# Attention by two key tiles, finer steps of maxima and recurrence, and TensorE's instructions chained in program order

## The chip, the cores and the metric

The kernel runs as one program on one core of a Trainium2 chip. The metric is the device time of one execution in microseconds. TensorE multiplies matrices, VectorE and ScalarE work on elements, GpSimd (POOL) helps with some, and SyncE's queue issues the DMA transfers. Products land in PSUM, where the kernel holds eight tiles of 128 x 512 float32, called banks here; everything else lives in SBUF.

## The reference, cut to what matters

The model has two layers over 256 context and 1024 latent tokens. In each layer three token mixers read the same projected input: a Fourier mix, grouped-query attention (8 query heads, 2 key heads, width 64), and a gated linear recurrence (4 heads, 64 x 64 state) run forward and backward. Their outputs are concatenated and go through one output projection and a SwiGLU FFN.

```python
def attend(q, k, v):
    s = jnp.einsum('bkgqd,bksd->bkgqs', q, k).astype(jnp.float32) * (HEAD_DIM ** -0.5)
    p = jax.nn.softmax(s, axis=-1).astype(v.dtype)
    return jnp.einsum('bkgqs,bksd->bkgqd', p, v)

    ...
    for l in range(DEPTH):
        ...
        fx = fourier_mix(col(ux, OFF_FOURIER, FOURIER_W), w_four[l])
        ax, ac = attention_group(ux, uc, base_c, q_norm[l], k_norm[l], tabs, ctx_out)
        rx, rc = hgrn_group(ux, uc, base_c, lb_all[:, l], hg_norm[l], ctx_out)
        x = x + g_a * (jnp.concatenate([fx, ax, rx], axis=-1) @ w_out[l])
```

Context tokens attend to context only, latent tokens to both; in the second layer the context has no output.

## The kernel before, in words

Tokens are cut into three chunks: chunk 0 is the context (256), chunks 1 and 2 are 512 latent tokens each. `mixers` first runs the projections of a layer and then the stretch that the change is about: attention, with the recurrence (`hgrn`) and the Fourier mix (`fourier`) interleaved.

Attention works in units: a unit is a pair of heads `j` and a chunk of queries. Layer 0 has 12 units (four of them context units with two key tiles), layer 1 has 8; a latent unit has ten key tiles of 128. For each key tile and each of the two heads `a`, two products make the scores (`sc`, L622 and L623, a float32 value split in two parts), ScalarE takes the exponential (`p`, L625), and one tile later the values are weighted (`pv`, L631). A float32 product appears as two instructions. The two heads of a weighting write the two halves of 64 partitions of one bank, so each uses 64 of TensorE's 128 columns. After every second tile four products with 32 columns each collect the sums (`sm`, L636). `unit_finish` divides by the sums.

The exponent needs the row maximum in advance. `unit_prepare` loads the queries of a unit two units ahead (`qf`, L567), converts them (four ScalarE instructions, L577 and L578), and for each block of 128 queries and each head multiplies with all keys in three pieces of 512, 512 and 256 columns (`mx`, L588) and reduces each piece on VectorE (`mp`, L589). The maxima are transposed (`mt`, L596) and brought into the operand `Q2` by a DMA (L603).

`hgrn` builds the recurrence by seven levels of doubling. A level multiplies small blocks (`lp`, 64 rows by 64 columns, L789), merges the result under a mask (VectorE, L796), and scales `W` and the keys (L813, L815) for the next level. Layer 0 has a second group of blocks for the context. Then states are summed (`kdt`, `kv`, `ST`) and read out (`ho`, L858 and L861, `oss`).

PSUM has four tags of two banks each: `mm`, `sc`, `mx`, `pv`. The finishing sum (L652) and `mt` share `mx` with the maxima.

The order of the work: each generator yields at the ends of its steps, and the loop in `mixers` interleaves them: for every key tile one step of the maxima of a later unit (three pieces) and 1.1 or 1.07 steps of `other`, the chain of two `hgrn` and one `fourier`. This gives each instruction a place in program order. A scheduler that works with modelled times then orders each engine's instructions: where the next one in program order is not ready by its model, it takes a later one that is. So TensorE's order in the trace is not program order: pieces of the recurrence and maxima stand between the parts of attention. At run time each engine works through its list in that fixed order.

Of the kernel before, what the change touches and what calls it, by code (L numbers as in the profile page):

```python
# [87 lines left out]
DELAY = 1  # L88
ORDER = (2, 3, 4, 6, 7, 0, 1, 5)
RATE = (1.1, 1.07)  # L90
# [4 lines left out]
PREPSTEPS = (5,)  # L95
# [5 lines left out]
class Kern:  # L101
    def __init__(self, ctx, tc, I, C, out):
# [9 lines left out]
        self.n = 0  # L112
# [14 lines left out]

    def mm3(self, out, terms, first=True, last=True):

        n = len(terms)  # L130
        for i, (lh, ll, rh, rl) in enumerate(terms):
            self.nc.tensor.matmul(out, lh, rh, start=(first and i == 0), stop=False)  # L132
            self.nc.tensor.matmul(out, lh, rl, start=False, stop=False)  # L133
            self.nc.tensor.matmul(out, ll, rh, start=False, stop=(last and i == n - 1))  # L134
# [11 lines left out]
    def consts(self):  # L146
# [9 lines left out]
        nc.tensor.transpose(ptr[:, 0:16], cv, self.c["ident"][0:16, 0:16])  # L156
# [15 lines left out]
    def vectors(self):  # L172
# [24 lines left out]
        nc.tensor.transpose(ptr[:, 0:P], rows, self.c["ident"])  # L197
# [33 lines left out]
    def ada_first(self, l, tags):  # L231
# [5 lines left out]
        for k in range(KD):  # L237
            if k == EARLYK:
                self.early_slabs(l)
            for q in range(4):  # L240
                t = next(tag)
                w = self.t2(f"wa{l}_{k}_{q}", tag=t, bufs={"wa": WAB, "pa": PAB, "acc": ACB}[t])
                nc.sync.dma_start(out=w, in_=self.I["w_ada"][l, k * P:(k + 1) * P, q * 512:(q + 1) * 512])
                nc.tensor.matmul(acc[32 * q:32 * q + 32], self.sc32[:, k, :], w, start=(k == 0), stop=(k == KD - 1))
# [3 lines left out]
    def ada_sums(self, l, blocks, tags):  # L248
# [19 lines left out]
        for group in groups:  # L268
# [16 lines left out]
            for r, acc in enumerate(accs):  # L285
                nc.tensor.matmul(ps[32 * r:32 * r + 32], self.c["ones"][:, 0:32], acc)
# [7 lines left out]
    def ada_columns(self, l, ps, group):  # L294
# [5 lines left out]
        for b in range(4):  # L300
            nc.tensor.transpose(pt[:, b * P:(b + 1) * P], rowsb[:, b * P:(b + 1) * P], self.c["ident"])
# [35 lines left out]
    def first_chunk(self, ci, vec):  # L337
# [20 lines left out]
        for t, xt in enumerate(xs):  # L358
# [9 lines left out]
            nc.tensor.matmul(R[:, t * P:(t + 1) * P], rb, self.c["ident"])  # L368
        for d in range(KD):
            pt = self.ps("mm", f"xtp{ci}_{d}")  # L370
            for t, xt in enumerate(xs):
                nc.tensor.transpose(pt[:, t * P:(t + 1) * P], xt[d // 4][:, d % 4 * P:d % 4 * P + P], self.c["ident"])
# [22 lines left out]
    def square_sum(self, acc, ci):  # L395
        n = CHUNKS[ci][1]
        ss = self.ps("pv", f"ss{ci}")
        self.nc.tensor.matmul(ss[:, :n], self.c["ones"], acc[:, :n])
# [62 lines left out]
    def qk_norm_rope(self, l, nm, ci, t0, n, acc, done):  # L461
# [7 lines left out]
        def rest():  # L469
            ss = self.ps("mx", "qss")  # L470
            nc.tensor.matmul(ss[:, :n], self.c["blkq"], sq[:, :n])
# [86 lines left out]
    def unit_prepare(self, l, i, j, ci, ops):  # L558
# [37 lines left out]
        nc.tensor.transpose(pt[:2 * nt, 0:P], m, self.c["ident"])  # L596
# [9 lines left out]
    def unit_attend(self, l, j, ci, Q1, Q2):  # L606
# [3 lines left out]
        g = j // 2  # L610
        n = CHUNKS[ci][1]
        nk = 2 if ci == 0 else 10
        pv = self.ps("pv", f"pv{j}_{ci}")
        sm = self.ps("pv", f"sm{j}_{ci}")
        ps = []
        for kt in range(nk + 1):
            if kt < nk:
                ks = slice(kt * P, (kt + 1) * P)
                p = []
                for a in range(2):  # L620
                    sc = self.ps("sc", "sc")
                    nc.tensor.matmul(sc[:, :n], self.K1[g][:, ks], Q1[a], start=True, stop=False)  # L622
                    nc.tensor.matmul(sc[:, :n], self.K2[g][0:66, ks], Q2[a][0:66], start=False, stop=True)  # L623
                    pf = self.t2(f"p{a}", tag="pa", bufs=PAB)[:, :n]
                    nc.scalar.activation(out=pf, in_=sc[:, :n], func=AF.Exp, scale=0.125)  # L625
                    p.append(pf)
                ps.append(p)
            if kt:
                i = kt - 1
                for a in range(2):  # L630
                    nc.tensor.matmul(pv[64 * a:64 * a + 64, :n], self.V[:, i, 64 * g:64 * g + 64], ps[i][a], start=(i == 0), stop=(i == nk - 1))  # L631
                if i % 2:
                    for a in range(2):
                        for o in range(2):
                            r = 64 * a + 32 * o
                            nc.tensor.matmul(sm[r:r + 32, :n], self.c["first"], ps[i - 1 + o][a], start=(i == 1), stop=(i == nk - 1), tile_position=(0, r))  # L636
            if kt == DELAY and self.pending:
                self.pending()
                self.pending = None
            yield  # L640
        if self.pending:
            self.pending()
        pvs, sms = [self.t2(nm, tag="acc", bufs=ACB)[:, :n] for nm in ("pvs", "sms")]
        nc.scalar.copy(out=pvs, in_=pv[:, :n])
        nc.scalar.copy(out=sms, in_=sm[:, :n])
        self.pending = lambda: self.unit_finish(j, ci, pvs, sms)

    def unit_finish(self, j, ci, pvs, sms):
# [3 lines left out]
        nc.tensor.matmul(sm[:, :n], self.c["blk"], sms)  # L652
# [56 lines left out]
    def hgrn(self, l, j):  # L709
# [10 lines left out]

        def load(src, name, a=0):
# [12 lines left out]
        for ci in cis:  # L734
# [3 lines left out]
            for dr in range(2):  # L738
                v.tensor_tensor(out=W[ci][:, 1 - dr], in0=f[dr][:, a:a + n], in1=q[:, a:a + n], op=ALU.mult)

# [4 lines left out]
        def pairs(group, product, put):  # L745

            lp = [self.ps("mm", "lp").rearrange("p (c t) -> p c t", t=64) for _ in range(2)]
            for x, (ci, c) in enumerate(group):
# [3 lines left out]
                if x == 3:  # L752
                    yield
# [3 lines left out]
            yield  # L757
# [536 lines left out]
```

## Time and profile before

| | us |
|---|---|
| median of 3 runs | 3320.73 (3320.39 to 3325.08) |
| the profiled execution | 3320.49, of which span 3318.6 |
| TensorE busy | 3238.2 (98%), 17370 products |
| VectorE busy | 1698.8 (51%) |
| ScalarE busy | 1116.6 (34%) |

Times of the trace are counted from the span's start. Busy time of TensorE is the union of its instructions; their ends are modelled and overlap the next instruction's start, so the cost of an instruction in a stream is the distance from its start to the next start. "Idle before" names the time an engine did nothing before an instruction and what ended it. The attention stretch of layer 0 lies from 350.5 to 779 us, that of layer 1 from 2094.8 to 2471.9 us.

### The profile page before, as it was taken

To read this page: it belongs to the slowest core of one execution; us is meant where nothing else is said; L and a number is where in the kernel's file an instruction comes from. 1 tells how busy PE (TensorE), PEld (TensorE's weight loads), DVE (VectorE), ACT (ScalarE), POOL (GpSimd) and SP (SyncE) were. 2 spreads that over 40 slices of the span, in tenths; PEclk is the share of its full clock that TensorE was granted. 3 is DMA by queue.
4 is the path that set the end of the run, shared out by engine and by line. 5 is a ranking of instruction groups with operands and counts; after the bars stand their busy time and mean duration, and the time that the engine had idled before them with its cause. 6 is when DMAs were issued, how large, how long until landed. Compare 5 with 4: busy or idle time off the path is not lost.

```text
span 3318.6 us, 43008 instructions
## 1 busy us (share of the span) xinstructions
PE 3238.2 (98%) x17370; PEld 2414.4 (73%) x17370; DVE 1698.8 (51%) x2980; ACT 1116.6 (34%) x2074; POOL 125.3 (4%) x100
## 2 busy tenths in 40 slices
PE   7999999999999999999999999999999999999999
PEld 4877544456788888888888787544448788888887
DVE  5298766652465353353335637677533533333344
ACT  5245555454321111111114635445552311111113
POOL 1000000000200000000001200000001100000000
PEclk9999999999999999999999999999999999999999
DMA  7346111024122141131112333111132111111112
GB/s 272 112 149 203 57 50 44 20 92 157 32 83 89 39 140 39 58 114 39 39 39 77 122 101 108 42 63 32 52 98 93 46 50 45 51 51 51 45 45 77
DMA packets 239647, 258.21 MB, mean 78 GB/s; under 512 B 13504, under 2 KB 175192, under 8 KB 239448
## 3 DMA queue, kind: packets, MB, share of 16 engines
q1 hardware_dynamic: 239448, 255.46, 24.3%
q8 instruction: 136, 2.23, 0.3%
q14 instruction: 63, 0.52, 0.0%
HBM read 207.29 MB, written 47.97 MB: 77 GB/s over the span
## 4 chain that ended last, share of the span: by engine, by line
PE 85%; DVE 6%; DMA 4%; ACT 3%; issue 2%; POOL 1%; SPq 0%; DVEq 0%; POOLq 0%; ACTq 0%
PE pv L631 6%; PE fd L132 5%; PE fd L133 5%; PE fd L134 5%; PE pg L134 5%; PE pg L132 5%; PE pg L133 5%; PE pu L132 5%; PE pu L134 5%; PE pu L133 5%; PE mx L588 3%; PE u L132 3%; PE sm L636 3%; PE u L133 3%; PE u L134 3%; PE sc L622 3%
## 5 line engine op out<-in xcount | busy, mean ns | idle before, releaser
L1033 DVE SCALAR_TENSOR_TENSOR xT<-fd,mod,xT 128x512 f32<-128x512 f32 (+1 forms) x448 | 292.8, 686 | 162.2 <-PE fd L134 162.2
L132 PE MATMUL pg<-mh,hw_gate 128*128 128x512 f32 (+1 forms) x880 | 326.9, 372 | 9.3 <-ACT hf L326 8.2
L133 PE MATMUL pg<-ml,hw_gate 128*128 128x512 f32 (+1 forms) x880 | 326.4, 371 | 1.7 <-POOL ml L328 0.8
L134 PE MATMUL pg<-mh,lw_gate 128*128 128x512 f32 (+1 forms) x880 | 326.4, 371 | 1.3 <-DVE lw_gate L126 1.1
L132 PE MATMUL pu<-mh,hw_up 128*128 128x512 f32 (+1 forms) x880 | 325.4, 370 | 0.8 <-ACT hw_up L125 0.8
L134 PE MATMUL pu<-mh,lw_up 128*128 128x512 f32 (+1 forms) x880 | 324.4, 369 | 1.4 <-DVE lw_up L126 1.4
L133 PE MATMUL pu<-ml,hw_up 128*128 128x512 f32 (+1 forms) x880 | 324.3, 369 | 0.0
L1066 DVE TENSOR_TENSOR sg<-pu,sg 128x512 f32<-128x512 f32 (+1 forms) x110 | 70.1, 637 | 489.7 <-PE pu L134 489.7
L589 DVE TENSOR_REDUCE mp<-mx 128x1 f32<-128x512 f32 (+1 forms) x400 | 223.8, 590 | 133.9 <-PE mx L588 132.3
L625 ACT ACTIVATE p<-sc 128x512 f32<-128x512 f32 (+1 forms) x336 | 186.1, 586 | 188.7 <-PE sc L623 185.0
L631 PE MATMUL pv<-p,V 128*64 128x512 f32 (+1 forms) x672 | 231.4, 606 | 0.0
L125 ACT CAST hw_gate<-rw_gate 128x512 fp32r<-128x512 f32 x92 | 54.6, 615 | 497.8 <-issue 370.5
L132 PEld LDWEIGHTS pg<-mh,hw_gate 128*128 128x128 f32 x880 | 167.1, 190 | 40.2 <-ACT hf L326 9.0
L278 DVE SCALAR_TENSOR_TENSOR as<-wa,sc,as 128x512 f32<-128x512 f32 x224 | 163.3, 757 | 55.6 <-DMA wa<-in_w_ada_dram 54.5
L134 PEld LDWEIGHTS pg<-mh,lw_gate 128*128 128x128 f32 x880 | 166.9, 190 | 31.6 <-DVE lw_gate L126 3.0
L133 PEld LDWEIGHTS pg<-ml,hw_gate 128*128 128x128 f32 x880 | 167.2, 190 | 30.5 <-DVE ml L331 1.3
L132 PEld LDWEIGHTS pu<-mh,hw_up 128*128 128x128 f32 x880 | 166.4, 189 | 31.4 <-ACT hw_up L125 1.9
L134 PEld LDWEIGHTS pu<-mh,lw_up 128*128 128x128 f32 x880 | 166.0, 189 | 29.3 <-DVE lw_up L126 1.6
L133 PEld LDWEIGHTS pu<-ml,hw_up 128*128 128x128 f32 x880 | 166.2, 189 | 27.3
L134 PE MATMUL fd<-ah,lwd 128*128 128x512 f32 (+1 forms) x448 | 164.0, 366 | 3.0 <-DVE lwd L126 3.0
L132 PE MATMUL fd<-ah,hwd 128*128 128x512 f32 (+1 forms) x448 | 164.3, 367 | 1.9 <-ACT ah L125 1.9
L132 PE MATMUL fd<-a,hwd 128*128 128x512 f32 (+1 forms) x448 | 165.0, 368 | 0.6 <-DVE xT L1033 0.6
(291 smaller groups left out, 6364.2 us busy)
## 6 DMA issues: line engine op xcount, KB each, us to landing
wa<-in_w_ada_dram SPq DMA_DIRECT2D x192, 256.0 KB
rw_gate<-in_w_gate_dram SPq DMA_DIRECT2D x46, 512.0 KB
rw_up<-in_w_up_dram SPq DMA_DIRECT2D x46, 512.0 KB
rwd<-in_w_down_dram SPq DMA_DIRECT2D x46, 512.0 KB
rwin<-in_w_in_dram SPq DMA_DIRECT2D x30, 512.0 KB
rwo<-in_w_out_dram SPq DMA_DIRECT2D x16, 512.0 KB
mixf<-dmix SPq DMA_DIRECT2D x32, 256.0 KB
dx<-x0T SPq DMA_DIRECT2D x8, 640.0 KB
```

The lines of the kernel that those rows point to most:

```text
L132: self.nc.tensor.matmul(out, lh, rh, start=(first and i == 0), stop=False)
L133: self.nc.tensor.matmul(out, lh, rl, start=False, stop=False)
L134: self.nc.tensor.matmul(out, ll, rh, start=False, stop=(last and i == n - 1))
L278: nc.vector.scalar_tensor_tensor(out=acc, in0=w, scalar=sc, in1=acc, op0=ALU.mult, op1=ALU.add)
L588: nc.tensor.matmul(mx[:, :kn], Q1[a][:, t * P:(t + 1) * P], self.K1[g][:, k0:k0 + kn])
L589: nc.vector.tensor_reduce(out=mp[:, a * nt + t, i:i + 1], in_=mx[:, :kn], axis=AX.X, op=ALU.max)
L622: nc.tensor.matmul(sc[:, :n], self.K1[g][:, ks], Q1[a], start=True, stop=False)
L625: nc.scalar.activation(out=pf, in_=sc[:, :n], func=AF.Exp, scale=0.125)
L631: nc.tensor.matmul(pv[64 * a:64 * a + 64, :n], self.V[:, i, 64 * g:64 * g + 64], ps[i][a], start=(i == 0), stop=(i == nk - 1))
L636: nc.tensor.matmul(sm[r:r + 32, :n], self.c["first"], ps[i - 1 + o][a], start=(i == 1), stop=(i == nk - 1), tile_position=(0, r))
L1033: self.nc.vector.scalar_tensor_tensor(out=x, in0=acc[:, :n], scalar=self.mod[l][:, vec, d, s:s + 1], in1=x, op0=ALU.mult, op1=ALU.add)
L1066: nc.vector.tensor_tensor(out=sg[:, :n], in0=pu[:, :n], in1=sg[:, :n], op=ALU.mult)
```

## The change

`unit_attend` becomes two functions: `unit_scores` makes the scores of one key tile, `unit_weigh` weights two key tiles at once and adds their sums. The loop in `mixers` goes through pairs of key tiles; the weighting of a pair comes one pair later, between the two score steps of the next pair. Between them stand two and then three steps of maxima (`MAXIMA`), and after both some 8.5 or 7.4 steps of `other` (`RATE`). The generators yield more often: the maxima after each piece (25 steps a latent unit, where there were 8), the recurrence after each VectorE group, and where something has to become ready it yields four empty steps (`lag`). What is computed stays the same. While `strict` is on, every TensorE instruction is made to follow the one before it in program order; ScalarE, VectorE and the DMA queue are ordered by the scheduler as before. Maxima may now run up to four units ahead.

```diff
-DELAY = 1
+MAXIMA = (2, 3)
+LAG = 4
-RATE = (1.1, 1.07)
+RATE = (8.5, 7.4)
-PREPSTEPS = (5,)
+PREPSTEPS = (0, 2, 4, 6)
...
+    def ordered(self, r):
+
+        if self.strict:
+            if self.last_pe is not None:
+                self.tc.add_manual_dep(r.ins, self.last_pe.name, mybir.DependencyInfo(
+                    mybir.DependencyClass.NoSync, mybir.DependencyReason.DATA), reason="order")
+            self.last_pe = r.ins
+
+    def mm(self, *args, **kw):
+        self.ordered(self.nc.tensor.matmul(*args, **kw))
...
                     mx = self.ps("mx", "mx")
-                    nc.tensor.matmul(mx[:, :kn], Q1[a][:, t * P:(t + 1) * P], self.K1[g][:, k0:k0 + kn])
+                    self.mm(mx[:, :kn], Q1[a][:, t * P:(t + 1) * P], self.K1[g][:, k0:k0 + kn])
                     nc.vector.tensor_reduce(out=mp[:, a * nt + t, i:i + 1], in_=mx[:, :kn], axis=AX.X, op=ALU.max)
-                yield
+                    yield
...
+    def unit_scores(self, u, kt):
...
+        tag = ("pa", "pa", "pa", "acc")[self.np % 4]
+        self.np += 1
+        for a in range(2):
+            sc = self.ps("sc", "sc")
+            self.mm(sc[:, :n], self.K1[g][:, ks], Q1[a], start=True, stop=False)
+            self.mm(sc[:, :n], self.K2[g][0:66, ks], Q2[a][0:66], start=False, stop=True)
+            pf = self.t2(f"p{a}", tag=tag, bufs={"pa": PAB, "acc": ACB}[tag])[:, :n]
+            nc.scalar.activation(out=pf, in_=sc[:, :n], func=AF.Exp, scale=0.125)
+            p.append(pf)
+        u["p"].append(p)
+
+    def unit_weigh(self, u, kt):
...
+        for i in (kt, kt + 1):
+            for a in range(2):
+                self.mm(pv[64 * a:64 * a + 64, :n], self.V[:, i, 64 * g:64 * g + 64], p[i][a], start=(i == 0), stop=(i == nk - 1))
+        for a in range(2):
+            for o in range(2):
+                r = 64 * a + 32 * o
+                self.mm(sm[r:r + 32, :n], self.c["first"], p[kt + o][a], start=(kt == 0), stop=(kt == nk - 2), tile_position=(0, r))
...
         def pairs(group, product, put):
...
                     for b in range(2):
                         product(lp[hh][hs[b], x], ci, c, hh, b)
-                if x == 3:
-                    yield
             c0 = CHUNKS[group[0][0]][0] // P
             for hh in range(2):
                 put(hh, slice(c0, c0 + len(group)), lp[hh][:, :len(group)])
-            yield
+                yield
...
                     v.tensor_tensor(out=w, in0=w, in1=g[:, fb:fb + mb, near:near + 1].to_broadcast([P, mb, m]), op=ALU.mult)
+                    yield
...
-            yield
+            yield from lag()
...
+        def maxima(k):
+
+            nonlocal nxt, ahead
+            while k:
+                if next(ahead, self) is not self:
+                    k -= 1
+                elif nxt < len(units) and done >= (0 if nxt == 3 else nxt - 4):
+                    ahead = prepare(nxt)
+                    nxt += 1
+                else:
+                    return
...
+        self.strict = True
+        for i, (j, ci) in enumerate(units):
...
+            for kt in range(0, u["nk"], 2):
+                self.unit_scores(u, kt)
+                maxima(MAXIMA[0])
+                finish, self.pending = self.pending, None
+                if last:
+                    weigh(*last)
+                self.unit_scores(u, kt + 1)
+                if finish:
+                    finish()
+                maxima(MAXIMA[1])
+                last = u, kt
                 credit += RATE[l]
                 while credit >= 1:
                     credit -= 1
                     next(other, None)
...
+        self.strict, self.last_pe = False, None
         self.out_proj(l)
```

## Rows read from the trace of the kernel before

**Rows 1.** Stretches: length, busy (x) of PE, PEld, DVE, ACT, POOL; clock, DMA.

```profile
350.50:779.00 428.50, 425.66 (x3026) 210.98 (x3025) 260.31 (x566) 221.59 (x407) 3.42 (x4) 1.00 0.15 47
2094.80:2471.90 377.10, 374.94 (x2564) 181.64 (x2562) 228.86 (x464) 192.09 (x332) 2.83 (x3) 1.00 0.15 46
770.00:800.00 30.00, 22.89 (x91) 12.41 (x90) 10.10 (x19) 13.93 (x29) 0.00 (x0) 0.89 0.53 173
```

**Rows 2.** Both attention stretches, `pv` (L631) alone, then `sm` (L636) alone: sums.

```profile
sum 805.60, PE 231.41 PEld 44.00; mean PE 115.71 PEld 22.00
...
sum 805.60, PE 109.78 PEld 16.09; mean PE 54.89 PEld 8.05
```

**Rows 3.** TensorE in order of time: start, busy us, engine, line, operation, tiles, count.

```profile
586.94 0.40 PE L588 MATMUL mx<-K,Qwh 128*128 128x512 f32 x1
587.27 0.46 PE L789 MATMUL lp<-W,kk 64*64 64x64 f32 x16
587.66 0.50 PE L622 MATMUL sc<-Qwh,K 128*128 128x512 f32 x1
588.00 0.28 PE L588 MATMUL mx<-K,Qwh 128*128 128x256 f32 x1
588.11 0.40 PE L623 MATMUL sc<-Qwl,K 66*128 66x512 f32 x1
588.35 0.39 PE L622 MATMUL sc<-Qwh,K 128*128 128x512 f32 x1
...
588.90 1.08 PE L631 MATMUL pv<-p,V 128*64 128x512 f32 x4
589.91 0.73 PE L588 MATMUL mx<-K,Qwh 128*128 128x512 f32 x2
...
591.50 1.07 PE L631 MATMUL pv<-p,V 128*64 128x512 f32 x2
...
598.05 0.69 PE L789 MATMUL lp<-W,kk 64*64 64x64 f32 x32
```

**Rows 4.** TensorE in order of time, at the end of layer 1's attention.

```profile
2468.26 1.94 PE L631 MATMUL pv<-p,V 128*64 128x512 f32 x8
2470.12 1.07 PE L636 MATMUL sm<-p,first 128*32 128x512 f32 x8
```

**Rows 5.** TensorE in order of time, maxima among layer 1's projections.

```profile
2080.49 0.62 PE L588 MATMUL mx<-K,Q 128*128 128x512 f32 x2
...
2081.40 0.39 PE L134 MATMUL u<-mh,lwin 128*128 128x512 f32 x1
2081.67 0.39 PE L588 MATMUL mx<-K,Q 128*128 128x256 f32 x1
```

**Rows 6.** VectorE's groups in layer 0's stretch: count, busy us, mean ns, idle before.

```profile
L589 DVE TENSOR_REDUCE mp<-mx 128x1 f32<-128x512 f32 x112 | 73.8, 686 | 49.8 <-PE mx L588 49.5
L589 DVE TENSOR_REDUCE mp<-mx 128x1 f32<-128x256 f32 x68 | 28.4, 419 | 19.0 <-PE mx L588 18.7
...
L796 DVE COPY_PREDICATED atc<-c_masks,lp 128x512 f32<-128x512 uint8 x24 | 16.1, 720 | 6.2 <-PE lp L789 6.2
```

**Rows 7.** SyncE's queue and VectorE in order of time, the Fourier input.

```profile
688.45 1.92 SPq L895 DMA_DIRECT2D uf<-du  x2
...
696.52 1.48 DVE L126 TENSOR_TENSOR ufl<-uf,ufh 128x1280 fp32r<-128x1280 f32 x1
```

**Rows 8.** TensorE in order of time, start of layer 0's output projection.

```profile
783.43 0.41 PE L132 MATMUL oacc<-mh,hwo 128*128 128x256 f32 x1
783.64 0.41 PE L133 MATMUL oacc<-ml,hwo 128*128 128x256 f32 x1
```

**Rows 9.** ScalarE and TensorE in order of time, query conversions and a transposition.

```profile
404.90 0.40 ACT L578 CAST Qwh<-qf 64x256 fp32r<-64x256 f32 x1
...
432.88 0.27 PE L596 MATMUL mt<-c_ident,mp 128*4 128x128 f32 x1
...
442.20 0.62 ACT L578 CAST Q<-qf 64x512 fp32r<-64x512 f32 x1
```

More of the change, by code (lines that the diff above doesn't have):

```diff
@@ L131, in mm3 @@
         for i, (lh, ll, rh, rl) in enumerate(terms):
-            self.nc.tensor.matmul(out, lh, rh, start=(first and i == 0), stop=False)
-            self.nc.tensor.matmul(out, lh, rl, start=False, stop=False)
-            self.nc.tensor.matmul(out, ll, rh, start=False, stop=(last and i == n - 1))
+            self.mm(out, lh, rh, start=(first and i == 0), stop=False)
+            self.mm(out, lh, rl, start=False, stop=False)
+            self.mm(out, ll, rh, start=False, stop=(last and i == n - 1))
     def exp_ln_set(self, after=None):
@@ L196, in vectors @@
         ptr = self.ps("mx", "ptr")
-        nc.tensor.transpose(ptr[:, 0:P], rows, self.c["ident"])
+        self.transpose(ptr[:, 0:P], rows, self.c["ident"])
         self.colv = self.cst.tile([P, P], F32, name="colv")
@@ L285, in ada_sums @@
             for r, acc in enumerate(accs):
-                nc.tensor.matmul(ps[32 * r:32 * r + 32], self.c["ones"][:, 0:32], acc)
+                self.mm(ps[32 * r:32 * r + 32], self.c["ones"][:, 0:32], acc)
             if SPREAD > 1:
@@ L397, in square_sum @@
         ss = self.ps("pv", f"ss{ci}")
-        self.nc.tensor.matmul(ss[:, :n], self.c["ones"], acc[:, :n])
+        self.mm(ss[:, :n], self.c["ones"], acc[:, :n])
         return ss
@@ L604, in unit_prepare @@
             nc.scalar.copy(out=Q2[a][64:66], in_=rows)
-    def unit_attend(self, l, j, ci, Q1, Q2):
+    def unit_scores(self, u, kt):
         nc = self.nc
[L610 to L639, printed above, removed]
-            yield
[L641 to L646, printed above, removed]
@@ new lines, in unit_scores @@
+        n, g = u["n"], u["j"] // 2
+        Q1, Q2 = u["ops"]
+        ks = slice(kt * P, (kt + 1) * P)
+        p = []
+        tag = ("pa", "pa", "pa", "acc")[self.np % 4]
[7 more added lines that the diff above has]
+            p.append(pf)
@@ new lines, in unit_scores @@
+        u["p"].append(p)
+    def unit_weigh(self, u, kt):
+        nc = self.nc
+        n, g, nk, p = u["n"], u["j"] // 2, u["nk"], u["p"]
+        if kt == 0:
+            u["pv"], u["sm"] = [self.ps("pv", f"{nm}{u['j']}_{u['ci']}") for nm in ("pv", "sm")]
+        pv, sm = u["pv"], u["sm"]
+        for i in (kt, kt + 1):
[5 more added lines that the diff above has]
+                self.mm(sm[r:r + 32, :n], self.c["first"], p[kt + o][a], start=(kt == 0), stop=(kt == nk - 2), tile_position=(0, r))
+        if kt == nk - 2:
+            pvs, sms = [self.t2(nm, tag="acc", bufs=ACB)[:, :n] for nm in ("pvs", "sms")]
+            nc.scalar.copy(out=pvs, in_=pv[:, :n])
+            nc.scalar.copy(out=sms, in_=sm[:, :n])
+            self.pending = lambda: self.unit_finish(u["j"], u["ci"], pvs, sms)
@@ L719, in hgrn, with lag @@
         hs = [slice(0, 64), slice(64, P)]
+        def lag():
+            for _ in range(LAG):
+                yield
         def load(src, name, a=0):
@@ L756, in pairs @@
                 put(hh, slice(c0, c0 + len(group)), lp[hh][:, :len(group)])
-            yield
+                yield
         def block(ci, c, b):
@@ L763, in own @@
         def own(out, ci, c, hh, b):
-            nc.tensor.matmul(out, kk[hs[hh], block(ci, c, b)], q[hs[hh], block(ci, c, b)])
+            self.mm(out, kk[hs[hh], block(ci, c, b)], q[hs[hh], block(ci, c, b)])
         for group in groups:
@@ L828, in hgrn @@
                         nc.scalar.copy(out=at[hh][hs[b], t0 // P:, hs[b]], in_=atc[hs[b], hh, t0 // P:])
-            yield
+            yield from lag()
         vt = self.five(f"vt{l}_{j}", shape=(P, 10, P))
@@ L865, in hgrn @@
             nc.scalar.activation(out=sq, in_=o[:, :n], func=AF.Square)
+            yield from lag()
             ss = self.ps("mm", "oss")
-            nc.tensor.matmul(ss[:, :n], self.c["blk"], sq)
+            self.mm(ss[:, :n], self.c["blk"], sq)
             rs = self.rstd(ss, n, 64, "ors")
+            yield
             v.tensor_tensor(out=sq, in0=o[:, :n], in1=rs[:, :n], op=ALU.mult)
@@ L1248, in mixers, with weigh @@
         other = itertools.chain(self.hgrn(l, 0), self.hgrn(l, 1), self.fourier(l))
-        credit = 0.0
-        self.pending = None
-        for i, u in enumerate(units):
-            ahead = prepare(i + AHEAD)
-            for _ in self.unit_attend(l, *u, *ops.pop(i)):
-                next(ahead, None)
+        self.pending = None
+        done = -1
+        nxt, ahead = AHEAD, iter(())
+        def maxima(k):
[8 more added lines that the diff above has]
+                    return
+        def weigh(u, kt):
+            nonlocal done
+            self.unit_weigh(u, kt)
+            if kt == u["nk"] - 2:
+                done = u["i"]
+        last = None
+        credit = 0.0
+        self.strict = True
+        for i, (j, ci) in enumerate(units):
+            while nxt <= i:
+                maxima(1)
+            u = {"i": i, "j": j, "ci": ci, "n": CHUNKS[ci][1], "nk": 2 if ci == 0 else 10, "p": []}
+            if nxt == i + 1:
+                for _ in ahead:
+                    pass
+            u["ops"] = ops.pop(i)
+            for kt in range(0, u["nk"], 2):
[9 more added lines that the diff above has]
+                last = u, kt
                 credit += RATE[l]
@@ L1258, in mixers @@
                     next(other, None)
-            for _ in ahead:
-                pass
+        weigh(*last)
         self.pending()
```

46 lines of the change are left out of this document (28 added, 18 removed).

## The prediction

> **What bounds the kernel now.** I read the busy times of the two stretches that the change touches, and then TensorE's instructions there in order of time. The attention stretches last 428.5 us in the first layer and 377.1 us in the second. [...]
>
> Time is counted start to start, since each instruction overlaps the next. Three costs of order can be read in [rows 3]. First, the two halves of a weighting step (`pv`, two heads, two instructions each) run beside each other if they stand together: four instructions are busy 1.08 us. If something stands between the halves, two instructions alone are busy 1.07 us, so a broken step costs double. Second, going from products over all 128 columns to products over 64 or 32 columns and back costs: a 512 column maximum takes 0.33 us before such a change (586.94 to 587.27) and a score 0.34 us after one (587.66 to 588.00), where one inside a run takes 0.24 us (588.11 to 588.35). That is 0.10 on each side, 0.20 us an entry. Third, a small run pays at its own ends: 16 small products are busy 0.46 us and 32 are busy 0.69, so 16 more cost 0.23; of the 0.39 us from 587.27 to 587.66 some 0.15 is overhead.
>
> **The change part by part.** Sums are against the profiled execution's 3320.5 us (span 3318.6, 1.9 around it), 0.2 us below the median of 3320.73.
>
> *Weighting by two key tiles.* `unit_weigh` puts eight `pv` and eight `sm` instructions side by side. Where that happens by chance now, they are busy 1.94 and 1.07 us [rows 4]. A layer has 40 such pairs of key tiles with 512 queries: 80 x 3.01 = 241 us for both. The context units of layer 0 (four, an estimated 1.7 us each from half the columns) add 7. Now the two lines are busy 231.41 + 109.78 = 341.2 us [rows 2], so 93 us go. Each run's end lies some 0.07 us over the next run (1.08 busy against 1.01 from 588.90 to 589.91 [rows 3]), and some 155 runs fewer give back 11. Gain 82.
>
> *Fewer entries.* Following TensorE's order through both stretches I count 178 and 150 entries from full width into narrow products, with [rows 3] as the pattern. Afterwards the order is fixed by the code, so I count it there. Each pair of key tiles enters once for the weighting (44 and 40). The recurrence's groups of products stand in one piece instead of being scattered: with the read-out 26 and 20 entries, where 4 of layer 0's second groups are cut off from their first by the end of a burst of steps. That leaves 70 and 60. 198 entries fewer at 0.20 are 39 us. Runs of small products fall from 90 and 61 to 26 and 20, at 0.15 us each 16 us. Gain 55. Together 137 us.
>
> *The chain.* TensorE now takes its instructions in program order, so an instruction that is not ready holds up everything behind it. Before, another one went first. Four such waits can be priced.
>
> (1) The second piece of a pair issues three maxima in a row into two banks. In [rows 5] the third maximum starts 1.18 us after the first (2080.49 to 2081.67), and the product before it was already stretched, to 0.27 us: that is the time for a bank to be computed, reduced and free. Issued back to back, the third is reached after some 0.46. The wait is 0.72 us; by the same sum it is 0.83 if the second is the narrow one, and 0.45 if the first is (its reduction takes 0.42 instead of 0.69 [rows 6]). A unit of 25 pieces meets this four times, 2.45 us; 7 units in layer 0 and 6 in layer 1 are prepared inside: 32 us.
>
> (2) In layer 0 a level has a second group, the context's. Its products need the two banks of the first group, which VectorE must have merged: two masked copies of 0.72 us [rows 6] and a few tenths of passing on, 1.75 us. Counting steps against the bursts of 8.5, 12 of the 16 second groups fall into the burst of their first: 9 at 1.75 and 3 that go by ScalarE at about 2, together 22 us. Layer 1 has no context group.
>
> (3) The finishing sum and the maxima's transposition use the same two banks as the maxima. 20 finishes at about 0.4 and 13 transpositions at 0.3, each the rest of one reduction: 12 us (bounds 0 and 24: none if the reader is free, twice if it has one more instruction in hand).
>
> (4) The Fourier part now comes in the last two or three bursts. Its input is loaded behind the recurrence's last store on SyncE's queue; the load is issued at 688.45, and the first split of what it brings ends at 698.0 [rows 7], 9.6 us later. From the recurrence's last sum of squares to that store stand two ScalarE and two VectorE instructions, about 2.7 us by the 0.69 of [rows 6]. TensorE has 2 us of other work meanwhile in layer 0 and an attention pair, 7 us, in layer 1. I take waits of 13 and 6, and 3 in each layer for the chain from the last `pq` to the transform: 25 us (bounds 6 and 45).
>
> The sum is 91 us. The finer pieces in the projections (`PREPSTEPS`) stand among full-width products, where [rows 5] shows a wait of 0.04; I cost them at nothing, and at 0.3 us for each of some 60 pieces (18 us) if VectorE has no room. The changed tag of every fourth pair of probabilities only moves a buffer, 0 to 2 us. The end of each stretch stays late in the same way: the last unit's copy, sum, store and load, now with the Fourier store beside it, 0 to 5 us a layer.
>
> 137 - 91 = 46, so **3274 us**.
>
> [...] In the trace the granted clock is 1.00 in both stretches, where TensorE hardly waits, and 0.89 across the end of the first, where it is busy for 22.89 of 30 us [rows 1]. [...]
>
> **Rivals.**
>
> *A: the waits are filled.* Each wait gives VectorE time to catch up, so later ones shrink; only the third maximum is forced by the order alone. Then 137 - 32 = 105, 3215 us. For it: VectorE is idle 39% of the time [rows 1]. Against it: (2) is a plain latency.
>
> *B: no gain.* VectorE serves one queue in order, and whatever it has in hand (0.4 to 0.7 us [rows 6]) stands before each reduction. At another 0.55 us a pair and 84 pairs, 46 us more: 3320. For it: its 260 us of work would fill 63% of a shorter stretch in layer 0. Against it: the same queue served TensorE without waits before.
>
> *C: slower, the head of each unit.* In the new order a unit's first maximum follows the transposition of the unit before it directly, with no step between its load, its four conversions and that maximum. If load and conversions are not done early, the chain stands. In the trace one unit's last conversion ended 9.9 us after the transposition of the context unit before it (432.88 to 442.82), while that context unit had its own done at 405.3, 27 us ahead of the same transposition [rows 9]. 16 units are prepared inside the stretches. At 9.9 us each it costs 159 us, 3433; it turns the forecast into a loss from 2.9 us a head on. Against it: the late one came behind a context unit with only four pieces, and there are three such places; other loads run ahead. If it happens at half the heads, 3353.
>
> *D: the chain does not bring what it says.* Only TensorE's instructions are chained. If ScalarE's exponentials come late, the weighting stands together but waits in front, and the 82 us become a wait: 3356. Against it: the weighting comes one pair behind its scores, some 8 us.
>
> [...]
>
> **How the numbers follow.** Forecast 0.48, its own range 3250 to 3300. A 0.20, B 0.14, C 0.10, D 0.03, E 0.05. B falls to faster and slower with 0.05 each and to same with 0.04. Faster than 3314 (0.2%, 6.6 us, about what a measurement of this kernel can tell from none) is 0.48 + 0.20 + 0.05 = 0.73. Same is B's 0.04 and 0.02 from the mild end of C: 0.06. The rest, 0.21, is slower. The range from 3205 to 3325 leaves out most of C, D and E (0.16) and a few hundredths below. Its low end is A with (1) a third smaller; its high end has the upper bounds of (3) and (4) and the projections' 18 us together.
>
> **What would show it.** Right: in the profile after, `pv` stands in runs of eight with `sm` behind it, and the two lines are busy about 248 us in all. The stretches last about 412 and 347 us (the parts above, by layer). TensorE's waits are named by the reductions of the maxima, by the masked copies in layer 0 and by the Fourier input. Wrong: `pv` runs of two remain, or exponentials are waited for (D); waits for the conversions of the queries at the head of units (C); a granted clock below 1.00 in the middle of the stretches (E); waits under 40 us in all (A) or over 130 (B).

## The result and the profile after

The change made the kernel slower: 3379.23 us median (3371.96 to 3382.30) against 3320.56, a ratio of 1.0174 with a 95% interval of 1.0161 to 1.0187. The forecast was 3274 us. The profiled execution took 3382.12 us with a span of 3380.2, 61.6 us more than before.

Two rows of the page of the kernel after, the busy tenths of TensorE and its granted clock in 40 slices, show where:

```profile
PE   7999888887999999999999999998989999999999
PEclk9999889898999999999999999999999999999999
```

The fifth to the tenth digit (a slice is 84.5 us) are layer 0's attention. TensorE was busy for over 99% of both stretches before, at a clock of 1.00 [rows 1], so that time could be gained only in its own instructions; now its digits in layer 0 are 8 and 7, and the clock is no longer full. The two stretches of the kernel after, cut as in [rows 1] (length; busy (x) of PE, PEld, DVE, ACT, POOL; clock; DMA share, GB/s):

```profile
345.98:833.76 487.78, 406.64 (x3026) 221.16 (x3026) 258.26 (x562) 220.80 (x407) 3.40 (x4) 0.90 0.13 41
2157.68:2533.53 375.85, 334.22 (x2556) 182.69 (x2554) 220.66 (x453) 191.33 (x332) 3.05 (x3) 0.95 0.14 44
```

Layer 0 went from 428.5 to 487.8 us, layer 1 from 377.1 to 375.9. Three things are to be read from these rows and [rows 1]. TensorE's idle time (length less busy) was 5 us and is 81.1 + 41.6 = 122.8. The clock was 1.00 and is 0.90 and 0.95; busy time times the missing share is 40.7 + 16.7 = 57 us, an estimate of what the clock alone cost. And busy time times the clock, an estimate of what the same list would take at a clock of 1.00, fell from 801 to 366.0 + 317.5 = 683.5: the new order saves 117 us. So the regrouping worked, and waits and the clock took back 118 + 57. That makes the two stretches 58 us longer; the other 3.6 of the 61.6 lie outside them.

The weighting's two lines in the kernel after, over the whole span (count | busy us, mean ns | idle before):

```profile
L140 PE MATMUL pv<-p,V 128*64 128x512 f32 (+1 forms) x672 | 176.6, 650 | 0.0
L140 PE MATMUL sm<-p,first 128*32 128x512 f32 (+1 forms) x672 | 90.1, 609 | 0.0
```

Together 266.7 us against 341.2 [rows 2], a part of it at a lower clock (0.50 in the run of eight at 583.37 below). L140 is the helper that issues every product. TensorE's waits in layer 0 of the kernel after (us in total, times, longest):

```profile
PE mx L140 <- DVE mp L606: 16.8, 30, 1.2
PE lp L140 <- DVE atc L815: 12.5, 17, 1.5
PE fo L140 <- DVE ycl L129: 6.6, 1, 6.6
PE pq L140 <- ACT ufh L128: 5.7, 1, 5.7
PE lp L140 <- ACT at L818: 4.1, 4, 1.3
PE mx L140 <- ACT ar L669: 3.6, 8, 0.6
PE kv L140 <- ACT kt L864: 3.6, 5, 1.2
PE mx L140 <- ACT Q L595: 3.5, 2, 1.9
PE sc L140 <- ACT Q L622: 3.0, 2, 1.9
...
PE mx L140 <- ACT Qwh L595: 2.7, 1, 2.7
```

The same view of layer 1:

```profile
PE mx L140 <- DVE mp L606: 16.8, 28, 1.0
PE pq L140 <- ACT za L969: 7.0, 2, 6.6
PE mx L140 <- ACT ar L669: 2.8, 5, 0.6
...
PE pq L140 <- ACT ufh L128: 2.1, 1, 2.1
```

`mp` is written by the reductions of the maxima, `atc` and `at` by the merges of the recurrence, `ar` by the reader of the finishing sum, `Q` and `Qwh` by the conversions of queries. `pq` and `fo` are products of the Fourier part, `ufh` its split input, `za` and `ycl` come from what it computes after that.

How a wait and the clock go together stands in TensorE's instructions in order of time, kernel after, layer 0:

```profile
574.51 0.50 PE L140 MATMUL mx<-K,Q 128*128 128x256 f32 x2 [1.59 <-ACT Q L595]
575.41 0.39 PE L140 MATMUL mx<-K,Q 128*128 128x256 f32 x1 [0.40 <-DVE mp L606]
575.73 1.16 PE L140 MATMUL lp<-hq,kk 64*64 64x64 f32 x64
578.04 1.17 PE L140 MATMUL lp<-hq,kk 64*64 64x64 f32 x16 [1.16 <-ACT atc L786]
...
579.74 0.63 PE L140 MATMUL sc<-Qwl,K 66*128 66x512 f32 x1
580.16 0.63 PE L140 MATMUL sc<-Qwh,K 128*128 128x512 f32 x1
...
583.37 3.68 PE L140 MATMUL pv<-p,V 128*64 128x512 f32 x8
```

In a row come a late query conversion, a third maximum, and the second group of the recurrence that waits for ScalarE's copy of the first. Then a score takes 0.42 us start to start (579.74 to 580.16) where it took 0.24 at a clock of 1.00 in the kernel before (588.11 to 588.35 [rows 3]), and a weighting run of eight is busy 3.68 us instead of 1.94 [rows 4]. The granted clock around it (same columns as the stretches):

```profile
563.00:577.00 14.00, 9.41 (x100) 4.57 (x98) 6.76 (x16) 8.79 (x18) 0.00 (x0) 1.00 0.14 42
577.00:589.00 12.00, 10.17 (x41) 4.13 (x42) 7.75 (x21) 5.70 (x12) 0.00 (x0) 0.57 0.07 17
589.00:603.00 14.00, 12.19 (x122) 6.91 (x121) 9.54 (x21) 6.74 (x13) 0.00 (x0) 1.00 0.01 2
```

TensorE was busy 9.41 of 14 us, then the clock was 0.57 in the mean of 12 us (0.50 in each 2 us from 579 to 587), then it was 1.00 again. Most of the waits were over by then (4.6 us in the first row, 1.8 in the second): what follows them pays a second time.

### The profile page after: what moved, and what is told of

Read it like the earlier page. It is cut to its first block, busy times and chain, and to the rows that moved or that the text cites. A ratio compares the mean times of both kernels' runs of the same rounds, so it can differ in the third digit from the quotient of the medians.

```text
span 3380.2 us, 42946 instructions
## 1 busy us (share of the span) xinstructions
PE 3179.7 (94%) x17370; PEld 2426.7 (72%) x17370; DVE 1695.3 (50%) x2980; ACT 1113.6 (33%) x2074; POOL 125.3 (4%) x100
## 4 chain that ended last, share of the span: by engine, by line
PE 77%; DVE 10%; DMA 6%; ACT 4%; issue 2%; POOL 0%; SPq 0%; DVEq 0%; POOLq 0%; ACTq 0%
PE fd L140 15%; PE pu L140 14%; PE pg L140 14%; PE u L140 8%; PE oacc L140 5%; PE sc L140 5%; PE pv L140 5%; DMA wa<-in_w_ada_dram 4%; PE sm L140 3%; PE mx L140 2%; PE v L140 2%; DVE mp L606 2%; DVE as L295 2%; DVE hf L341 1%; PE lp L140 1%
## 5 line engine op out<-in xcount | busy, mean ns | idle before, releaser
L140 PE MATMUL pg<-mh,hw_gate 128*128 128x512 f32 (+1 forms) x880 | 326.7, 372 | 9.3 <-ACT hf L343 8.2
L140 PE MATMUL pg<-mh,lw_gate 128*128 128x512 f32 (+1 forms) x880 | 326.4, 371 | 1.9 <-DVE lw_gate L129 1.8
L140 PE MATMUL pg<-ml,hw_gate 128*128 128x512 f32 (+1 forms) x880 | 326.6, 371 | 1.7 <-POOL ml L345 0.8
L140 PE MATMUL pu<-mh,lw_up 128*128 128x512 f32 (+1 forms) x880 | 324.4, 369 | 2.6 <-DVE lw_up L129 2.5
L140 PE MATMUL pu<-mh,hw_up 128*128 128x512 f32 (+1 forms) x880 | 325.2, 370 | 0.8 <-ACT hw_up L128 0.8
L140 PE MATMUL pu<-ml,hw_up 128*128 128x512 f32 (+1 forms) x880 | 324.1, 368 | 0.0
L140 PE MATMUL fd<-a,hwd 128*128 128x512 f32 (+1 forms) x896 | 255.6, 368 | 0.5 <-DVE xT L1060 0.5
L140 PEld LDWEIGHTS pg<-mh,hw_gate 128*128 128x128 f32 x880 | 167.1, 190 | 40.0 <-ACT hf L343 8.9
L140 PEld LDWEIGHTS pg<-mh,lw_gate 128*128 128x128 f32 x880 | 167.0, 190 | 32.4 <-DVE lw_gate L129 3.9
L140 PEld LDWEIGHTS pg<-ml,hw_gate 128*128 128x128 f32 x880 | 167.2, 190 | 30.4 <-DVE ml L348 1.2
L140 PEld LDWEIGHTS pu<-mh,hw_up 128*128 128x128 f32 x880 | 166.4, 189 | 31.2 <-ACT hw_up L128 1.9
L140 PEld LDWEIGHTS pu<-mh,lw_up 128*128 128x128 f32 x880 | 165.9, 189 | 30.8 <-DVE lw_up L129 3.2
L140 PEld LDWEIGHTS pu<-ml,hw_up 128*128 128x128 f32 x880 | 166.1, 189 | 27.5
L140 PEld LDWEIGHTS fd<-a,hwd 128*128 128x128 f32 x896 | 161.4, 189 | 30.4 <-DVE xT L1060 3.0
L140 PE MATMUL pv<-p,V 128*64 128x512 f32 (+1 forms) x672 | 176.6, 650 | 0.0
L140 PE MATMUL fd<-ah,lwd 128*128 128x512 f32 (+1 forms) x448 | 164.5, 368 | 4.2 <-DVE lwd L129 4.2
```

The source lines that it names most:

```text
L140: self.ordered(self.nc.tensor.matmul(*args, **kw))
```

## Experiments

Each is timed against the kernel before on the same chip; its median there was between 3313 and 3321 us, so ratios are compared. For each, the two stretches are shown with the columns used above (in one case layer 0 alone). The expectations count the waits up to 836 and 2536 us, a little past the stretches, and so speak of 126 us of idle time where 122.8 lie inside. Theory W: the strict chain's waits cost twice, once as idle time and once by the clock. Its rivals are named as they come.

**The chain left out.** `self.strict = True` becomes `False`, nothing else.

> The kernel after, with the chain of TensorE's instructions left out; loops, pieces and the order in which they are written stay. Theory W (the chain's waits cost twice: as idle time, and because the granted clock falls after them): idle time of the two stretches goes from 126 us back to under 10, the clock to 1.00, and a part of the regrouping is lost again; 3290 to 3330 us. Theory G (the new loops cost the time: bursts of 8.5 steps, LAG, finer pieces): waits and low clock stay, over 3360.

```profile
346.24:783.20 436.96, 417.27 (x3009) 218.75 (x3009) 261.50 (x568) 220.52 (x413) 3.41 (x4) 0.97 0.15 46
2100.64:2475.50 374.86, 359.72 (x2537) 185.79 (x2536) 225.41 (x459) 193.80 (x337) 3.05 (x3) 0.97 0.14 45
```

3323.30 us, ratio 1.0016 (1.0006 to 1.0026). With the same loops and pieces the time is nearly that of before, so Theory G falls as the cause of the loss. W has its time, but not all its details: 35 us of idle time stay, and the clock is 0.97. The same stretches without their last 49 and 40 us:

```profile
346.24:733.71 387.47, 385.88 (x2859) 191.58 (x2858) 236.59 (x533) 199.49 (x377) 3.41 (x4) 1.00 0.13 39
2100.64:2435.25 334.61, 332.49 (x2422) 163.63 (x2421) 202.57 (x427) 174.49 (x306) 3.05 (x3) 1.00 0.12 39
```

Up to there TensorE idles for 3.7 us in all and the clock is 1.00. The other 31 us and all of the lower clock stand at the end, where the Fourier part is left over. So the Fourier part's waits do not hang on the chain: they come with the new loops, and to that extent G holds.

**Useless work in the waits.** Products with a zero matrix, added into the weighting's open bank.

```diff
+    def fill(self, k):
+        if self.open:
+            u = self.open
+            for _ in range(k):
+                self.mm(u["pv"][:, :u["n"]], self.zero, self.K1[u["j"] // 2][:, 0:u["n"]], start=False, stop=False)
...
+            if group[0][0] == 0:
+                self.fill(6)
...
+                if l == 0 and k == 1 and MAXIMA[1] == wide[0]:
+                    self.fill(2)
```

> The kernel after, with 128 more products of zero weights added into the open weighting bank in layer 0, in front of products that waited: six before the recurrence's second group, two before the third maximum of a row. They are 128 x 0.24 = 31 us of work that computes nothing. Theory W: they stand where TensorE was idle (some 25 us of 83), the granted clock of the stretch rises from 0.90 to 0.95 or more, and the kernel gets faster in spite of them, 3350 to 3370. Theory N (the clock falls since narrow products stand in long runs, whatever the waits): the clock stays at 0.90 and the kernel is not faster, 3380 to 3395.

```profile
349.84:826.96 477.12, 415.34 (x3150) 235.88 (x3150) 258.50 (x562) 220.53 (x407) 3.41 (x4) 0.94 0.13 42
2150.66:2526.20 375.54, 333.91 (x2555) 183.42 (x2554) 220.73 (x453) 191.74 (x332) 3.04 (x3) 0.96 0.14 45
```

3363.56 us, ratio 1.0140 (1.0124 to 1.0157): faster than the change, with some 30 us of work more (the trace has 124 of the 128 products expected; 124 x 0.24 is an estimate). Busy time in layer 0 rose by only 8.7 us, since the clock rose from 0.90 to 0.94, and idle time fell from 81 to 62. This is W's forecast, a little short of its 0.95. But the added products also break up the long runs of small ones, so theory N is not yet out.

**No runs of small products.** The recurrence's groups become two full-width products each.

```diff
-            for x, (ci, c) in enumerate(group):
-                for hh in range(2):
-                    for b in range(2):
-                        product(lp[hh][hs[b], x], ci, c, hh, b)
+            for hh in range(2):
+                self.mm(lp[hh][:, :len(group)], self.K1[0][:, 0:P], self.K1[0][:, 0:64 * len(group)].rearrange("p (c t) -> p c t", t=64))
```

> The kernel after, with each group of the recurrence's 64 x 64 products replaced by two full-width products that fill the same two banks (these products of the recurrence are left out). No long run of the smallest products is left, the waits for the merges stay. TensorE has some 45 and 35 us less to do. Theory W: idle time in layer 0 stays at 70 us or more and the time at the lower clock at 60 us or more; about 3300 us. Theory N: the time at the lower clock falls under 25 us; about 3260 us.

```profile
346.80:808.36 461.56, 381.02 (x1810) 202.89 (x1810) 256.02 (x562) 219.16 (x406) 3.40 (x4) 0.91 0.14 43
2134.21:2492.92 358.71, 317.22 (x1564) 170.17 (x1562) 220.93 (x453) 191.31 (x332) 3.12 (x3) 0.96 0.14 46
```

3339.39 us, ratio 1.0078 (1.0063 to 1.0093). Idle time stays at 80.5 us and the clock at 0.91 in layer 0 without a single long run of small products. Theory N falls. Both times were too low: busy time times the clock fell by 19 and 13 us, not 45 and 35, so the small products in their runs had been cheap.

**A shorter merge.** The masked copy takes one block, `lp[:, 0:1]`, into `atc[:, hh, c1]` with `c1` one block wide.

> The kernel after, with the masked copies of the recurrence merging one of eight blocks (the rest of the merge is left out; TensorE's list and order are the same, so the runs of 80 small products stand as they do). The copies take a fraction of their 0.72 us, so that the wait between the two groups of layer 0 (12.5 us in all) shrinks to under 6 us and VectorE has 20 us less to do. Theory W (the clock falls after waits): time at the lower clock in layer 0 falls from 99 us to 65 or less; 3345 to 3365 us. Theory N (it falls since narrow products stand in long runs): it stays at 85 us or more; 3365 to 3378 us.

```profile
346.22:810.17 463.95, 389.51 (x3026) 215.35 (x3026) 244.90 (x562) 219.99 (x407) 3.40 (x4) 0.93 0.14 43
2127.44:2500.09 372.65, 331.04 (x2556) 181.32 (x2554) 209.75 (x453) 191.71 (x332) 3.05 (x3) 0.96 0.14 45
```

3351.57 us, ratio 1.0110 (1.0095 to 1.0125), inside W's range. TensorE's list and order are unchanged. Idle time in layer 0 fell by only 6.7 us, but busy time by 17: of the stretch's gain the larger part came back through the clock (0.90 to 0.93).

**The second group later.**

```diff
-RATE = (8.5, 7.4)
+RATE = (10.0, 7.4)
...
-            for group in groups:
+            for x, group in enumerate(groups):
+                if x:
+                    yield from lag()
                 yield from pairs(group, level, put)
```

> The kernel after, with four steps between the two groups of a level in layer 0 (RATE 10.0 in place of 8.5, since 64 steps are added). Theory W: the waits for the masked copies (16 us) go, and with them the low clock that follows them, for some 4 us of more changes between full-width and narrow products; 3340 to 3360 us, clock of the stretch 0.95 or more. Theory N: the runs of narrow products are hardly shorter, the clock stays near 0.90; 3365 to 3375.

```profile
347.40:803.43 456.03, 386.52 (x3027) 215.12 (x3026) 256.25 (x562) 220.63 (x407) 3.40 (x4) 0.93 0.14 44
2127.15:2499.45 372.30, 329.79 (x2555) 180.80 (x2554) 220.72 (x453) 191.18 (x332) 3.05 (x3) 0.97 0.14 45
```

3345.19 us, ratio 1.0083 (1.0068 to 1.0098), inside W's range, though the clock rose to 0.93 and not to 0.95. With the computation whole, one wait taken out of layer 0 gives 32 us there, 12 of them idle time.

**Maxima one by one.** Five slots in a pair of key tiles, one maximum each; the recurrence stays in bursts. Each unit's query load and conversions are done one unit ahead (`coming`).

```diff
-                self.unit_scores(u, kt)
-                maxima(MAXIMA[0])
+                for _ in self.unit_scores(u, kt):
+                    slot()
                 finish, self.pending = self.pending, None
                 if last:
                     weigh(*last)
-                self.unit_scores(u, kt + 1)
-                if finish:
-                    finish()
-                maxima(MAXIMA[1])
+                slot()
+                for a, _ in enumerate(self.unit_scores(u, kt + 1)):
+                    if a and finish:
+                        finish()
+                    slot()
```

> The kernel after, with the maxima one by one in the five slots of spread (and its early query loads), but the recurrence in bursts of 8.5 and 7.4 steps at the end of a pair as in after. Theory W: of the 126 us of idle time the maxima's part goes (33 + 6 + 4 us, and 9 for the heads of units), and a part of the low clock behind it; the recurrence's and the Fourier's waits stay: 3315 to 3340 us. Theory V: the burst of the recurrence fills VectorE's queue and the maxima wait behind it all the same: over 3355.

```profile
344.04:800.65 456.61, 396.32 (x3028) 215.49 (x3028) 262.00 (x563) 225.00 (x408) 3.41 (x4) 0.90 0.14 44
2121.35:2477.55 356.20, 327.77 (x2558) 179.07 (x2556) 223.29 (x454) 195.29 (x332) 2.94 (x3) 0.96 0.15 47
```

3319.11 us, ratio 1.0010 (0.9997 to 1.0022): the loss is gone, by W's number. Idle time fell by 21 and 13 us and busy time by 10 and 6, but the clock in layer 0 stayed at 0.90, although the waits for the reductions, 16.8 us, are no longer among the seven largest there, the least of which is 2.9 us. The waits inside the bursts of the recurrence, which this kernel keeps, may be what holds it; no run shows that by itself.

**Maxima and recurrence in slots.** `slot()` also does `credit += RATE[l] / 5` and as many steps of the recurrence.

> The kernel after, with maxima and recurrence in five slots of a pair of key tiles (after each head's scores and after the weighting), one maximum and 1.7 or 1.5 steps a slot, and each unit's query load and conversions one unit ahead of its maxima. The chain stays. Theory W: hardly a third maximum meets a full bank, the second groups come one slot later, heads are ready; idle time falls from 126 us to about 40, the clock to 0.98 or more, some 10 us of more changes of width; 3235 to 3270 us. Theory V (VectorE's queue in order is the limit: waits move but stay): idle over 90 us, 3330 or more. Theory N: idle falls but the clock stays near 0.90 in layer 0; about 3300.

```profile
345.96:761.76 415.80, 374.20 (x3029) 208.74 (x3028) 260.32 (x564) 223.25 (x408) 3.41 (x4) 0.95 0.15 48
2084.50:2443.60 359.10, 329.64 (x2557) 177.62 (x2556) 224.52 (x454) 194.28 (x332) 2.95 (x3) 0.96 0.15 47
```

3289.40 us, ratio 0.9913 (0.9898 to 0.9928), faster than before. V gave 3330 and more and falls. W's range ended 19 us lower: 71 us of idle time are left, not 40, and the clock is 0.95 and 0.96. N's time of about 3300 is as near, but N had the clock near 0.90 in layer 0.

**The Fourier part's waits.** Empty steps in it, first in the change alone (RATE 9.1 and 8.0), then in the kernel with slots (RATE 9.5 and 8.3).

```diff
             U.append((uh, ul))
+        yield from lag(3)
...
             dft += [hi, lo]
-        yield
+            yield from lag(4)
...
                 self.split(pq(kt * P), Yh[:, kt], Yl[:, kt])
+            yield from lag(5)
...
```

> The kernel after with nothing changed but the Fourier part: the empty steps of spread2 in it, and RATE 9.1 and 8.0 to make up for them. Theory W: its waits (15 us in layer 0, 12 in layer 1) and the 19 us at the lower clock beside them go, all other waits stay: 3345 to 3360 us. Rival: with the Fourier part stretched over more pairs the ends of the stretches stay late by as much: 3372 to 3385.

> The kernel of spread with two further waits taken out: 23 and 17 empty steps inside the Fourier part (after its input split, after the first sums, after the two splits of the sums), so that attention stands between a split and the products that read it, with RATE 9.5 and 8.3; and the maxima of the second unit that the projections leave over go into the slots instead of one row. In spread the Fourier waits were 15 and 12 us, 30 us of busy time passed at the lower clock beside them, and the row at the start of layer 1 waited 5 us. Theory W: these go, 25 + 15 + 9 us; 3240 us (3230 to 3260), clock of both stretches 0.98 or more. Theory V: VectorE's and ScalarE's queues hold the same work, the waits come back elsewhere; 3280 or more.

In the change alone, layer 0:

```profile
346.19:828.70 482.51, 406.76 (x3026) 222.09 (x3026) 257.66 (x562) 221.47 (x407) 3.41 (x4) 0.90 0.13 41
```

3374.94 us, ratio 1.0172 (1.0157 to 1.0187): no gain clear of noise; W missed and the time is in its rival's range. Idle time fell by only 5 us, and the clock stayed at 0.90. The faster rate also makes every burst larger; whether that is the reason is not shown. In the kernel with slots:

```profile
346.99:756.91 409.92, 373.33 (x3029) 208.18 (x3028) 260.41 (x564) 223.50 (x408) 3.41 (x4) 0.96 0.16 49
2075.20:2430.05 354.85, 328.15 (x2558) 178.77 (x2556) 224.31 (x454) 194.29 (x332) 2.95 (x3) 0.97 0.15 49
```

3274.15 us, ratio 0.9868 (0.9852 to 0.9883): 15 us of the 49 expected, between W and V. With every product in its written place, 63 us of idle time stay.

**The same without the chain.** `self.strict = False`.

> The kernel of spread2 with the chain left out. Theory W: the order is then made by the list scheduler again, which breaks some of the weighting runs (34 + 32 of 84 are left whole or nearly so in its order); few waits, clock near 1.00, but 20 to 60 us of the regrouping lost: 3275 to 3310. Theory P (in a well-spread program the chain adds nothing but waits): as fast as spread2 or faster.

```profile
345.58:750.09 404.51, 400.83 (x3026) 210.03 (x3026) 261.32 (x564) 223.88 (x407) 3.40 (x4) 1.00 0.16 49
2068.78:2413.27 344.49, 341.38 (x2557) 178.20 (x2555) 224.01 (x454) 194.61 (x332) 2.94 (x3) 1.00 0.15 49
```

3261.37 us, ratio 0.9831 (0.9815 to 0.9848). Theory P was right, and W's range was too high. Here idle time is 6.8 us and the clock 1.00, while busy time is 742 us: the chain's order would save 742 - 677 = 65 us (busy times clock against the kernel with it), and its waits and clock cost more.

**A looser order.** The 16 instructions of a weighting stay chained; what is written before them comes before, what is written behind comes behind; between two weightings TensorE's order is free. First with slots, then with the loops of the change as they are.

```diff
         if self.strict:
+            before = self.seg if self.weighing else []
+            if self.last_pe is not None and not before:
+                before = [self.last_pe]
+            for x in before:
+                self.tc.add_manual_dep(r.ins, x.name, ...)
+            if self.weighing:
+                self.last_pe, self.seg = r.ins, []
+            else:
+                self.seg.append(r.ins)
```

> The kernel of spread2 with a looser order in place of the chain: the 16 products of a weighting are chained among themselves and behind all that is written before them, everything written after them comes behind them, and between two weightings the list scheduler is free. Theory W: the weighting runs of spread2 (255 us for both lines, against 313 without the chain), with most of the waits filled, since another product of the same pair can go first; clock 0.99 or more; 3225 to 3250 us. Rival Q: each weighting now waits for the last product of its pair, 84 times, and the gain goes there; 3260 or more.

```profile
347.25:745.15 397.90, 372.09 (x3026) 207.85 (x3026) 260.87 (x564) 222.45 (x407) 3.40 (x4) 0.97 0.16 51
2059.67:2406.84 347.17, 324.76 (x2556) 177.68 (x2555) 223.98 (x454) 193.50 (x332) 2.94 (x3) 0.99 0.15 50
```

3255.42 us, ratio 0.9825 (0.9809 to 0.9842), the lowest here, but not apart from the kernel without any chain (0.9831). The weighting's two lines over the whole span:

```profile
L146 PE MATMUL pv<-p,V 128*64 128x512 f32 (+1 forms) x672 | 164.9, 613 | 0.0
L146 PE MATMUL sm<-p,first 128*32 128x512 f32 (+1 forms) x672 | 88.1, 596 | 0.0
```

It keeps the weighting's gain and pays 48 us of waits for it: between W and rival Q.

> The kernel after with the same looser order in place of the chain, nothing else changed (MAXIMA, LAG, RATE, bursts as in after). Theory W: of the chain's 126 us of waits most are filled, the clock comes back; 3250 to 3290 us. Rival Q: the maxima in a row and the bursts stand in one pair with few others to go first; over 3320 us.

```profile
349.66:774.59 424.93, 385.27 (x3026) 213.93 (x3026) 257.47 (x562) 219.44 (x407) 3.40 (x4) 0.96 0.15 47
2091.55:2448.35 356.80, 333.42 (x2555) 182.21 (x2553) 220.46 (x453) 191.11 (x332) 3.04 (x3) 0.97 0.15 47
```

3296.05 us, ratio 0.9945 (0.9930 to 0.9959), a few us above W's range. This is the most direct test of the cause: same pieces, same bursts, same weighting runs (in both traces all 84 have their eight `pv` side by side); only the order between weightings is free, and the change turns from 1.7% slower into 0.5% faster. Idle time falls from 123 to 63 us and the clock rises to 0.96 and 0.97. The weighting runs, which use 64 or 32 columns, are therefore not by themselves what lowers the clock.

## Why the prediction was wrong

Its sum was 137 - 91. Step by step:

- *Weighting by two key tiles*: right. Forecast 248 us for both lines; with the clock at 0.97 and 0.99 the looser order has 164.9 + 88.1 = 253.
- *Fewer entries*: a little too large. In TensorE's order after stand 79 and 66 entries, not 70 and 60; 15 at 0.20 are 3 us. The whole gain of order is 117 us instead of 137; with at most 5 from the weighting, some 12 us of the shortfall stay without a row.
- *The chain, waits (1) and (3)*: right. Forecast 32 + 12; measured 16.8 + 16.8 for the reductions, 3.6 + 2.8 for the finishing sum, and some 5 for the transpositions and sums.
- *Wait (2)*: 22 forecast, 12.5 + 4.1 measured.
- *Wait (4)*: 25 forecast, about 27 measured, but that is luck. The input was to cost 13 + 6 and cost 6.0 + 2.6 (`ufh` and its second half); what comes behind it was to cost 3 + 3 and cost 9 + 9 (`ycl`, `za` and the last splits). And without the chain the Fourier part still idles TensorE for 31 us, so this term belongs to the loops.
- *Not priced*: waits inside the recurrence and its read-out (`kv`, `kdt`, `ho`, `oss`, `kk`), which are latencies like (2) although LAG puts four empty steps in between, because those steps come in one burst; some 20 us. And the heads of the units, rival C's mechanism: 3.5 + 3.0 + 2.7 us, not 159.

The step that failed is the price of a wait. "The chain" counted every wait at its own length and left the clock at 1.00. The four waits named came out within a few us in the sum, (4) by luck, yet beside the 123 us of idle time the clock cost an estimated 57 more. Against the forecast of -46, 20 us less gain, 27 us more idle time (118 more than before, 91 forecast), 57 of the clock and 3.6 outside make +62. So the clock is the largest of the errors, a little over half of them.

This was rival E, a clock below 1.00 in the middle of the stretches, set at 0.05. The missing shares of the clock, 0.10 of 487.8 and 0.05 of 375.9, are an estimated 135 us at the 0.50 shown above, or 16% of both stretches. The chance was wrong, and so was its place: it was a rival instead of the companion of every wait in the sum. Inside its stretches the kernel before waited 5 us in all, so the rows there could hardly show whether the clock falls behind short waits. One place could: TensorE in order of time, kernel before, at the end of layer 0's stretch:

```profile
778.98 1.13 PE L652 MATMUL sm<-sms,c_blk 128*128 128x512 f32 x2 [0.70 <-ACT sms L645]
781.75 0.38 PE L132 MATMUL oacc<-mh,hwo 128*128 128x256 f32 x1 [1.64 <-ACT mh L125]
782.51 0.38 PE L133 MATMUL oacc<-ml,hwo 128*128 128x256 f32 x1 [0.38 <-DVE ml L126]
```

Waits of 0.70, 1.64 and 0.38 us come together here, and right behind them, from 783.43 on, a 256 column product takes 0.21 us start to start (783.43 to 783.64 [rows 8]) against 0.11 inside a run (588.00 to 588.11 [rows 3]); the granted clock was 0.98 from 781 to 783 us and 0.50 in each 2 us from 783 to 789. So waits of this length with a fallen clock behind them were on record.

With the chain the clock was 0.90 and 0.95, without it 1.00 up to the Fourier part. What stays open: how much idle time, and where, lowers the clock. It is not in proportion. One by one, the maxima gave 21 us of idle time back in layer 0, with most of the waits for their banks, and nothing of the clock (0.90); the shorter merge gave 7 back and the clock rose to 0.93.

## What to carry to other kernels

Before an engine that never waits is tied to a written order, every latency that its scheduler had been hiding has to be listed, and on TensorE each is to be priced above its length if the clock falls behind it: here 123 us of idle time came with a clock of 0.90 and 0.95, an estimated 57 us more. Chain only what must stand together, and leave the rest free to fill the waits. And if producer and consumer must be in written order, spread the pieces evenly: empty steps inside one burst keep nothing apart.

## What the runs showed of the hardware

In the place followed above, the clock fell from 1.00 to 0.50 after 14 us in which TensorE was busy for 9.41 and no wait was longer than 1.94 us. At 0.50 a weighting run of eight was busy 3.68 us, at 1.00 (568.86, same trace) 1.94. And 124 products that compute nothing, an estimated 30 us of work by the 0.24 of a score [rows 3], made the kernel some 11 us faster (1.0140 against 1.0174), while the clock of layer 0 rose from 0.90 to 0.94.
